# Stores of the FFN's left sums in GpSimd's queue, a residual in two steps, x ahead of single k tiles of weights, and half of tile six's offset by an adding transfer

## The chip, the cores and the metric

The kernel runs on one NeuronCore of one Trainium2 chip. The time is the device time of one execution in microseconds (us); before the change it is 1409.3 us, the median of three runs (1408.26 to 1409.47). Lower is better. Five engines work beside each other, each through its own instructions in order: TensorE (PE in the profile, with PEld for its weight loads), VectorE (DVE), ScalarE (ACT), GpSimd (POOL) and SyncE (SP), which here does nothing but issue DMAs. GpSimd issues some DMAs as well.

## The reference, cut to what matters

One layer of a transformer trunk over 1024 tokens of 1024 channels, in float32. Two attention branches share one input projection, are gated and merged, and a SwiGLU FFN follows; each half ends with a layer norm of a residual sum.

```python
def layer_norm(x, g, b):
    mu = jnp.mean(x, axis=-1, keepdims=True)
    var = jnp.mean(jnp.square(x - mu), axis=-1, keepdims=True)
    return (x - mu) * lax.rsqrt(var + LN_EPS) * g + b

h = x @ w_in                                   # q, k, v of both branches, and two gates
...
mix = (gate_a * y_a + gate_b * y_b) @ w_out
x = layer_norm(DEEPNORM_ALPHA * x + mix, ln1_g, ln1_b)
g, u = jnp.split(x @ w_ffn_in, 2, axis=-1)     # 1024 x (2 * 2816)
ffn = (jax.nn.silu(g) * u) @ w_ffn_out
x = layer_norm(DEEPNORM_ALPHA * x + ffn, ln2_g, ln2_b)
```

## The kernel before

**How a product is made.** Every matrix product runs in a reduced float format in three passes: each float32 operand is split in a high part (ScalarE's copy, a CAST in the profile) and a low part (VectorE subtracts the high part from the source), and TensorE multiplies high by high, high by low and low by high. `split` at lines 108 to 111 is this pair of instructions, so L110 and L111 stand for all splits, and a tile's name tells which. Most products are besides done as 2 by 2 blocks with seven instead of eight block products, from sums and differences of the operand's blocks; the seven steps of a column tile are `p1`, `p2`, `p6`, `p5`, `p7`, `p3`, `p4` in `pair_steps`. Each is 12 matmuls of 128 x 512. `p1`, `p6`, `p7` and `p4` add up in one PSUM bank (`sx`), and between them ScalarE copies the bank out: L202 after `p1`, L211 after `p6`. `p7` can't start until the copy at L211 is done.

**The start.** Column tile 0 of queries and of keys (`project_plain`) is done without the seven products, since its first operands are the first data to arrive. SP issues, in the order of the code, the weights of two k tiles (`w0raw`, 128 x 512) and then x of these two k tiles (`xraw`, 128 x 512 each, the low half of the tokens), four times over, and then the high halves of x. The splits on ScalarE and VectorE are kept in the same order by `in_order`, and TensorE runs k tile by k tile: six matmuls for each.

**The FFN's first product.** `up_steps(f)` makes the column tile f of the hidden layer, f from 1 to 21, and `run_pairs` runs their steps in turn; between two steps it prepares the weights of the next tiles (`right_f`: the sums `taf`, `tbf` and the splits `wbf`, `waf`, `wcf`; `left_f`: the split `wlf`, two tiles ahead). After every second f the two tiles of the hidden layer form a pair q = f // 2, and `left_sums(q)` lists pieces that prepare the second product's left operands: seven operands, each split into a tile `sl` and stored to DRAM (`s_dr`), with four sums between them. `next_piece` takes one piece after each step. The stores are issued by SP, as the loads of the weights are. `sl` takes a buffer of the tag `op` (8 buffers) three times in four, which it shares with `wlf` and `wcf`, and of the tag `kp` (4 buffers) otherwise. A buffer is free again when its store has landed.

**The residual.** Of tile q the scaled residual is built in DRAM: `x1_dr` is filled with the norm's offset at first, and `scale_x1(q, half)`, a piece of its own in the list, loads the normed half tile and the gain (`x1g`, tag `kp`), multiplies them on GpSimd and adds the product to `x1_dr` by an adding DMA. All five are instructions of GpSimd's queue, one behind the other; the multiply (L1362) waits for both loads to land.

**The end.** The second product adds up eight tiles of 128 tokens (`accumulate`, L1595), VectorE takes each sum down from PSUM (L1571) and makes the statistics of the norm (L1208, L1216), GpSimd raises the variance to the power -1/2 (L1217), and `norm_2` applies the norm: VectorE's L1606 subtracts the mean and multiplies by the gain. For tiles six (`x_6`, turn 1, j = 2) and seven VectorE's L1609 multiplies by 1/deviation and adds the offset; for others ScalarE and GpSimd do that. Tile seven's last product is cut in two column pieces of 256 (`d` and `dlast`).

**What sets the order.** Within an engine the framework places the instructions when it builds the program; in the code's order where `in_order` or a chain asks for it, and otherwise by when it reckons them ready. So an edit in one place can move rows elsewhere, and the rows of the built programs tell where each instruction stands.

## Time and profile before

One execution was profiled. Its own time is 1409.1 us; the span from the first to the last instruction that the trace shows is 1407.3 us, and 1.8 us lie around it.

| | |
|---|---|
| time, median of 3 runs | 1409.3 us |
| the profiled execution's own time | 1409.1 us |
| its span | 1407.3 us |
| mean granted TensorE clock | 0.998 |
| DVE busy | 1022.8 us (73%) |
| ACT busy | 716.8 us (51%) |
| POOL busy | 304.9 us (22%) |
| DMA moved | 306.98 MB, mean 218 GB/s |
| of it by GpSimd's queue (q0) | 19.93 MB |
| stores `s_dr<-sl`, issued by SP | 77 of 512 KB |

A row of the profile's timeline reads: start in us, duration in us, engine, line, operation, output <- inputs, shape, how many instructions are merged in the row; and in brackets the time that the engine stood idle before it, with what ended the wait. In other views `x77: 675/685/1782` is a count with the shortest, median and longest duration in ns. "SPq" and "POOLq" stand for the engines' issue of a DMA.

### The profile page before, as it was taken

The numbers are of one execution on the slowest core, as the hardware profiler recorded it, in microseconds if no ns is written. First come the engines' busy times: TensorE is split into PE (matmuls) and PEld (weight loads), VectorE is DVE, ScalarE is ACT, GpSimd is POOL, SyncE is SP. The second block draws the span as 40 slices with busy tenths as digits, with TensorE's granted clock in tenths as the row PEclk, the third lists the DMA queues.
The fourth block names the chain that finished last, engine by engine and source line by source line (L and its number), as shares of the span: only waits on it lengthen the run. The fifth ranks groups of instructions, "written<-read, shape, count | busy, mean of one in ns | idle before, by whom it ended". The sixth has DMA issues, their size and how long they took to land. (4 is left out here: it accounts for less than half of the span.)

```text
span 1407.3 us, 19064 instructions
## 1 busy us (share of the span) xinstructions
PE 1394.2 (99%) x6618; PEld 1160.4 (82%) x6618; DVE 1022.8 (73%) x1653; ACT 716.8 (51%) x1265; POOL 304.9 (22%) x400
## 2 busy tenths in 40 slices
PE   9999999999999999999999999999999999999997
PEld 7878888888888888888888888888888888888886
DVE  8967657545787878977887967767767665947666
ACT  6534344545888788873467644433444443323220
POOL 0000000002555878850122011112111100000032
PEclk9999999999999999999999999999999999999999
DMA  7476567847677478845774556556565539996652
GB/s 255 165 279 231 179 225 299 296 182 253 207 220 207 137 265 264 271 169 191 213 179 140 148 169 206 191 161 218 181 218 192 180 145 342 412 387 236 238 183 90
DMA packets 105665, 306.98 MB, mean 218 GB/s; under 512 B 10833, under 2 KB 27217, under 8 KB 105569
## 3 DMA queue, kind: packets, MB, share of 16 engines
q1 hardware_dynamic: 97824, 285.84, 57.0%
q0 software_dynamic: 7744, 19.93, 6.8%
q8 instruction: 52, 0.85, 0.2%
q14 instruction: 45, 0.36, 0.1%
HBM read 197.69 MB, written 108.56 MB: 218 GB/s over the span
## 5 line engine op out<-in xcount | busy, mean ns | idle before, releaser
L1595 PE MATMUL d<-wd,sl 128*128 128x512 f32 (+1 forms) x924 | 207.7, 387 | 0.0
L1595 PEld LDWEIGHTS d<-wd,sl 128*128 128x128 f32 x924 | 172.3, 188 | 35.4
L110 ACT CAST wd<-wd 128x512 fp32r<-128x512 f32 x77 | 46.0, 621 | 115.3 <-PE d L1595 82.1
L799 POOL TENSOR_TENSOR w_b<-w_b,kp_b 128x511 f32<-128x511 f32 (+3 forms) x96 | 96.1, 1013 | 24.8 <-DVE kp_b L794 18.3
L1571 DVE SCALAR_TENSOR_TENSOR x<-d,x 128x512 f32<-128x512 f32 (+1 forms) x57 | 38.6, 679 | 59.2 <-PE d L1595 59.2
L1217 POOL TENSOR_TENSOR mv<-mv,neghalf 128x1 f32<-128x1 f32 x16 | 15.4, 962 | 285.1 <-DVE mv L1216 280.5
L111 DVE TENSOR_TENSOR sl<-h,sl 128x512 fp32r<-128x512 f32 x77 | 53.3, 700 | 27.1 <-ACT sl L110 27.1
L110 ACT CAST sl<-h 128x512 fp32r<-128x512 f32 x77 | 46.6, 620 | 49.5 <-DMA s_dr<-sl 23.6
L794 DVE TENSOR_TENSOR_SCAN kp_b<-kp_b,ident_ps 128x512 f32<-128x512 f32 (+2 forms) x64 | 56.6, 885 | 20.8 <-ACT kp_b L791 19.8
L1417 PE MATMUL ops<-woh,m 128*128 128x512 f32 x224 | 69.8, 390 | 0.0
L734 POOL MEMSET bias<- 64x64 f32 x2 | 0.3, 144 | 315.0 <-ACT bias L730 315.0
L791 ACT ACTIVATE kp_b<-sc_b 128x512 f32<-128x512 f32 (+3 forms) x96 | 48.4, 504 | 27.9 <-PE sc_b L711 22.0
L111 DVE TENSOR_TENSOR wd<-wd,wd 128x512 fp32r<-128x512 f32 x77 | 52.9, 711 | 5.2 <-ACT wd L110 5.1
L111 DVE TENSOR_TENSOR pt_b<-tp_b,pt_b 128x512 fp32r<-128x512 f32 (+1 forms) x96 | 49.9, 544 | 6.6 <-ACT pt_b L110 5.7
L1360 POOL DMA_DIRECT2D x1g<-n_dr x16 | 9.2, 573 | 203.4 <-DVE wbf2l L111 31.6
L764 POOL TENSOR_SCALAR w_a<-w_a,st_a 128x640 f32<-128x640 f32 (+2 forms) x64 | 42.2, 666 | 48.8 <-PE sc_a L711 26.9
L183 PE MATMUL szf<-x1S73h,wcf 128*128 128x512 f32 x160 | 52.5, 389 | 0.0
L110 ACT CAST pt_b<-tp_b 128x512 fp32r<-128x512 f32 (+1 forms) x96 | 46.6, 503 | 8.0 <-PE tp_b L822 7.7
L1417 PEld LDWEIGHTS ops<-woh,m 128*128 128x128 f32 x224 | 42.1, 188 | 8.6
L759 ACT ACTIVATE w_a<-w_a,st_a 128x640 f32<-128x640 f32 (+2 forms) x64 | 44.7, 700 | 8.5 <-DVE st_a L753 7.1
L792 ACT ACTIVATE w_b<-sc_b 128x511 f32<-128x511 f32 (+3 forms) x96 | 48.3, 504 | 0.0
L822 PE MATMUL tp_b<-ident,w_b 128*128 128x128 f32 x288 | 47.3, 272 | 0.3
(1528 smaller groups left out, 4293.3 us busy)
## 6 DMA issues: line engine op xcount, KB each, us to landing
s_dr<-sl SPq DMA_DIRECT2D x77, 512.0 KB, 4.3
sl<-s_dr SPq DMA_DIRECT2D x77, 512.0 KB, 7.4
wLf<-in_w_ffn_in_dram SPq DMA_DIRECT2D x22, 512.0 KB, 5.8
wRf<-in_w_ffn_in_dram SPq DMA_DIRECT2D x22, 512.0 KB, 3.7
wd<-in_w_ffn_out_dram SPq DMA_DIRECT2D x22, 512.0 KB, 8.1
v_dr<-vc SPq DMA_DIRECT2D x16, 512.0 KB, 3.2
qs<-q_dr SPq DMA_DIRECT2D x16, 512.0 KB, 6.1
kh<-k_dr SPq DMA_DIRECT2D x16, 512.0 KB, 6.2
```

The source lines that it names most:

```text
L110: return (nc.scalar.copy(dst_h, src), nc.vector.tensor_tensor(dst_l, src, dst_h.bitcast(F32), ALU.subtract))
L111: nc.vector.tensor_tensor(dst_l, src, dst_h.bitcast(F32), ALU.subtract))
L183: mm(acc, lw[:, ks], rx, start=(first and kt == i == 0), stop=(kt == 3 and i == 2), skip_group_check=not first)
L759: nc.scalar.activation(s[:, 0:w], s[:, 0:w], AF.Exp, bias=st[:, m:m + 1], scale=-1.0, accum_out=st[:, 2:3])
L764: nc.gpsimd.tensor_scalar(s[:, 0:w], s[:, 0:w], st[:, 3:4], 0.0, ALU.mult, ALU.add)
L791: nc.scalar.activation(kp[:, c0:e], sc[:, 0:n], AF.Sigmoid, scale=-1.0)
L792: nc.scalar.activation(be[:, m0:e], sc[:, m0 - c0:n], AF.Sigmoid)
L794: nc.vector.tensor_tensor_scan(kp[:, 0:e], kp[:, 0:e], ident_ps()[:, 0:e], 0.0, ALU.mult, ALU.add)
L799: nc.gpsimd.tensor_tensor(be[:, m0:e], be[:, m0:e], kp[:, m0 - 1:e - 1], ALU.mult)
L822: ins = tr(tp[:, (qb - lo_q) * P:(qb - lo_q + 1) * P], wt[qb - q0][:, (kb - qb) * P:(kb - qb + 1) * P], ident)
L1417: mm(accs[j], a, b, start=(first and i == n == 0), stop=(i == 3 and n == 2), skip_group_check=not first)
L1595: mm(part, a, b, start=(fresh and i == k == 0), stop=(i == n - 1 and k == 2), skip_group_check=not fresh)
```

## The change

The diff has three parts; line numbers after it are higher by 15 to 46.

```diff
     for j in range(4):
+        if j == 0:
+            x_in((0,), LO)
+            for n in range(2):
+                dma(w0raw[0][:, n * 2 * P:(n + 1) * 2 * P], w_first[0][:, n * 2 * P:(n + 1) * 2 * P])
+            x_in((1,), LO)
+            continue
         dma(w0raw[j // 2][:, (LO, HI)[j % 2]], w_first[j])
...
-        in_order(split(*(t[:, cs] for t in w0hl[j // 2]), w0raw[j // 2][:, cs]))
-        for k in (2 * j, 2 * j + 1):
-            in_order(split_x(k, LO))
+        w = [t[:, cs] for t in (*w0hl[j // 2], w0raw[j // 2])]
+        if j == 0:
+            w0, w1 = ([t[:, n * 2 * P:(n + 1) * 2 * P] for t in w] for n in range(2))
+            in_order((nc.vector.tensor_copy(xh[0][:, LO], x_part(0, LO)),
+                      nc.scalar.copy(w0[0], w0[2])))
+            for hi, lo, src in ((xh[0][:, LO], xl[0][:, LO], x_part(0, LO)), w0):
+                in_order((nc.vector.tensor_tensor(lo, src, hi.bitcast(F32), ALU.subtract),))
+            in_order(split(*w1))
+        else:
+            in_order(split(*w))
+            in_order(split_x(2 * j, LO))
+        in_order(split_x(2 * j + 1, LO))
...
-    h_tiles, pieces = {}, []
+    h_tiles, pieces, last_store = {}, [], []
...
-        t, queue = slot("kp", f"x1g{tt}_{cs.start}"), nc.gpsimd
-        queue.dma_start(t[:, LO], n1_dr[tt][:, cs])
-        queue.dma_start(t[:, HI], rows_of(ln1_g, cs))
-        queue.tensor_tensor(t[:, LO], t[:, LO], t[:, HI], ALU.mult)
-        queue.dma_start(x1_dr[tt][:, cs], t[:, LO], accum_op=ALU.add)
+        box, queue = [], nc.gpsimd
+
+        def load():
+            t = slot("kp", f"x1g{tt}_{cs.start}")
+            box.append(t)
+            queue.dma_start(t[:, LO], n1_dr[tt][:, cs])
+            queue.dma_start(t[:, HI], rows_of(ln1_g, cs))
+
+        def scale():
+            t, = box
+            with tc.issue_after(last_store[0].ins):
+                queue.tensor_tensor(t[:, LO], t[:, LO], t[:, HI], ALU.mult)
+            queue.dma_start(x1_dr[tt][:, cs], t[:, LO], accum_op=ALU.add)
+        return load, scale
...
-                dma(s_dr[g][p][:, i * 1024:(i + 1) * 1024], o.bitcast(F32))
+                last_store[:] = [nc.gpsimd.dma_start(s_dr[g][p][:, i * 1024:(i + 1) * 1024],
+                                                     o.bitcast(F32))]
...
         if q < 8:
-            todo[5:5] = [lambda: scale_x1(q, LO)]
-            todo.append(lambda: scale_x1(q, HI))
+            for at, step in zip((1, 4, 6, 9), (*scale_x1(q, LO), *scale_x1(q, HI))):
+                todo[at] = part(both, todo[at], step)
...
+    def norm_2_split(tt, n):
+        (g, b), t, mv = norm2, acc_t[tt], statistics(f"2_{tt}", n)
+        rows = out[tt * P:(tt + 1) * P]
+        nc.vector.scalar_tensor_tensor(t, t, mv[:, 0:1], g, ALU.subtract, ALU.mult)
+        nc.scalar.activation(t[:, HI], t[:, HI], AF.Copy, scale=mv[:, 2:3])
+        nc.gpsimd.dma_start(rows[:, HI], t[:, HI], accum_op=ALU.add)
+
+        def rest():
+            nc.vector.scalar_tensor_tensor(t[:, LO], t[:, LO], mv[:, 2:3], b[:, LO],
+                                           ALU.mult, ALU.add)
+            dma(rows[:, LO], t[:, LO])
+        return rest
...
+            tied("p", nc.gpsimd.dma_start(out[6 * P:7 * P, HI], rows_of(ln2_b, HI)))
...
-            accumulate(END, j, ((0, 256), (256, HW)), lambda: mark_2(tt, 2, 0, 256))
+            accumulate(END, j, ((0, 256), (256, HW)), lambda: (mark_2(tt, 2, 0, 256), rest()))
```

**At the start**, x of k tile 0 is loaded first, then the weights of k tile 0 and of k tile 1 as two transfers of 128 x 256, then x of k tile 1; the weights' columns are laid out anew to suit (on the host and in `part`). VectorE instead of ScalarE makes the high part of x's k tile 0. On VectorE the first rows before are these:

```order
L267 MEMSET warm_182 128x256
L111 TENSOR_TENSOR w0l0_208<-w0raw0_205,w0h0_207 128x512
L111 TENSOR_TENSOR xl0_190<-xraw0_174,xh0_189 128x512
L111 TENSOR_TENSOR xl1_192<-xraw1_176,xh1_191 128x512
L111 TENSOR_TENSOR w0l0_208<-w0raw0_205,w0h0_207 128x512
L111 TENSOR_TENSOR xl2_194<-xraw2_178,xh2_193 128x512
```

On VectorE the same rows of the change:

```order
L267 MEMSET warm_182 128x256
L305 CAST xh0_189<-xraw0_174 128x512
L308 TENSOR_TENSOR xl0_190<-xraw0_174,xh0_189 128x512
L308 TENSOR_TENSOR w0l0_208<-w0raw0_205,w0h0_207 128x256
L111 TENSOR_TENSOR w0l0_208<-w0raw0_205,w0h0_207 128x256
L111 TENSOR_TENSOR xl1_192<-xraw1_176,xh1_191 128x512
L111 TENSOR_TENSOR w0l0_208<-w0raw0_205,w0h0_207 128x512
L111 TENSOR_TENSOR xl2_194<-xraw2_178,xh2_193 128x512
```

One cast has come in, and the first weight split is in two halves, the first of them behind x's low part; from `xl1` on the order is as before.

**In the FFN**, the 77 stores `s_dr<-sl` are issued by GpSimd. `scale_x1` no longer is two pieces of the list of 13: its load and its multiply ride on the pieces 1, 4, 6 and 9 of a list of 11, and the multiply is placed behind the latest store. On ScalarE, in tile f = 8 with the pieces of q = 3 (`h8` and `gt8` belong to f = 8; `wcf10` and `wlf11h` are weights for f = 10 and 11; `sl3_p` is the operand p of q = 3), these rows stand before:

```order
L110 CAST sl3_2_9318<-h7_9104 128x512
L110 CAST waf9h_9205<-taf9_9195 128x1024
L110 CAST wcf10_9353<-wRf10_9337 128x512
L211 COPY h8_9250<-sxf8_9178 128x512
L215 COPY gt8_9191<-szf8_9253 128x512
L110 CAST sl3_7_9356<-h6_8960 128x512
L110 CAST wlf11h_9377<-wLf11_9375 128x1024
```

On ScalarE at the same place of the change:

```order
L110 CAST sl3_2_9307<-h7_9116 128x512
L110 CAST waf9h_9208<-taf9_9198 128x1024
L110 CAST sl3_5_9273<-h7_9116 128x512
L211 COPY h8_9256<-sxf8_9181 128x512
L110 CAST sl3_7_9328<-h6_8966 128x512
L215 COPY gt8_9194<-szf8_9259 128x512
L110 CAST wcf10_9363<-wRf10_9347 128x512
L110 CAST wlf11h_9384<-wLf11_9382 128x1024
```

`sl3_7` has moved ahead of L215, and `wcf10` behind both. On GpSimd the rows of q = 3 before, all of them:

```order
L1360 DMA x1g3_0_9284<-n1_dr3_130 128x512
L1361 DMA x1g3_0_9284<-in_ln1_g_dram 128x512
L1362 TENSOR_TENSOR x1g3_0_9284<-x1g3_0_9284 128x512
L1363 DMA x1_dr3_138<-x1g3_0_9284 128x512
L1360 DMA x1g3_512_9431<-n1_dr3_130 128x512
L1361 DMA x1g3_512_9431<-in_ln1_g_dram 128x512
L1362 TENSOR_TENSOR x1g3_512_9431<-x1g3_512_9431 128x512
L1363 DMA x1_dr3_138<-x1g3_512_9431 128x512
```

On GpSimd the middle of q = 3 in the change:

```order
L1379 DMA x1g3_0_9219<-n1_dr3_130 128x512
L1380 DMA x1g3_0_9219<-in_ln1_g_dram 128x512
L1379 DMA x1g3_512_9311<-n1_dr3_130 128x512
L1404 DMA s_dr0_5_145<-sl3_5_9273 128x1024
L1385 TENSOR_TENSOR x1g3_0_9219<-x1g3_0_9219 128x512
L1404 DMA s_dr0_2_144<-sl3_2_9307 128x1024
L1386 DMA x1_dr3_138<-x1g3_0_9219 128x512
L1380 DMA x1g3_512_9311<-in_ln1_g_dram 128x512
L1404 DMA s_dr0_7_148<-sl3_7_9328 128x1024
L1404 DMA s_dr0_6_147<-sl3_6_9388 128x1024
```

The stores stand between the residual's loads, its multiply and its adding DMA, and the second half's load has come ahead of the first half's multiply.

**At the end**, the right half of tile six's rows of the output is filled with the norm's offset early on; ScalarE multiplies this half by 1/deviation, and an adding DMA of GpSimd's adds it to the output. VectorE keeps the left half, as an instruction of 128 x 512 placed between tile seven's two column pieces. VectorE's rows before, from the gain of tile six on:

```order
L1606 SCALAR_TENSOR_TENSOR x1_6_11163<-x1_6_11163,mv2_6_12737,ln2g_12180 128x1024
L1571 SCALAR_TENSOR_TENSOR x1_7_11164<-d1_1_3_12029,x1_7_11164 128x256
L1609 SCALAR_TENSOR_TENSOR x1_6_11163<-x1_6_11163,mv2_6_12737,ln2b_12182 128x1024
L1208 BN_STATS bn2_7_12713<-x1_7_11164 128x6
L1571 SCALAR_TENSOR_TENSOR x1_7_11164<-dlast_12763,x1_7_11164 128x256
```

VectorE's rows at the same place of the change:

```order
L1635 SCALAR_TENSOR_TENSOR x1_6_11166<-x1_6_11166,mv2_6_12741,ln2g_12183 128x1024
L1600 SCALAR_TENSOR_TENSOR x1_7_11167<-d1_1_3_12032,x1_7_11167 128x256
L1640 SCALAR_TENSOR_TENSOR x1_6_11166<-x1_6_11166,mv2_6_12741,ln2b_12185 128x512
L1223 BN_STATS bn2_7_12717<-x1_7_11167 128x6
L1600 SCALAR_TENSOR_TENSOR x1_7_11167<-dlast_12769,x1_7_11167 128x256
```

The order is the same; the third row is half as wide.

More of the change, by code (lines that the diff above doesn't have):

```diff
@@ L347, in part @@
         def part(side, half, k, first, last):
-            o = (k // 2 % 2) * HW + side * 2 * P + (k % 2) * P
+            o = (k // 2 % 2) * HW + (k % 2) * 2 * P + side * P
             wh, wl = (t[:, o:o + P] for t in w0hl[k // 4])
@@ L1357, in scale_x1, with both @@
     def scale_x1(tt, cs):
-        t, queue = slot("kp", f"x1g{tt}_{cs.start}"), nc.gpsimd
-        queue.dma_start(t[:, LO], n1_dr[tt][:, cs])
-        queue.dma_start(t[:, HI], rows_of(ln1_g, cs))
-        queue.tensor_tensor(t[:, LO], t[:, LO], t[:, HI], ALU.mult)
-        queue.dma_start(x1_dr[tt][:, cs], t[:, LO], accum_op=ALU.add)
+        box, queue = [], nc.gpsimd
[10 more added lines that the diff above has]
+        return load, scale
+    def both(*steps):
+        for step in steps:
+            step()
     def left_sums(q):
@@ L1665, in hybrid_trunk_kernel @@
             mark_2(tt, 1, 0, HW)
-            norm_2(tt, 2, j > 0)
+            if j == 2:
+                rest = norm_2_split(tt, 2)
+            else:
+                norm_2(tt, 2, j > 0)
 def granules(w):
@@ L1679, in layout @@
     w_in = granules(arr["w_in"])
-    w_first = np.stack([w_in[n].reshape(P, 4, 2 * P) for n in (0, 4)], axis=2)
+    w_first = np.stack([w_in[n].reshape(P, 4, 2, P) for n in (0, 4)], axis=3)
     w_v = np.stack([arr["w_in"][:, c:c + HW] for c in (1024, 2560)], axis=1)
```

2 lines of the change are left out of this document (1 added, 1 removed).

## The prediction

> **What bounds the kernel now.** I read the busy shares first, then TensorE's waits.
>
> ```profile
> PE 1394.2 (99%) x6618; PEld 1160.4 (82%) x6618; DVE 1022.8 (73%) x1653; ACT 716.8 (51%) x1265; POOL 304.9 (22%) x400
> PE sxp L183 <- ACT c L202: 1.3, 1, 1.3
> PE sxf L183 <- ACT h L211: 1.1, 2, 0.8
> PE sxp L183 <- DVE c L198: 0.4, 1, 0.4
> ```
>
> TensorE is busy 99% of the span and its clock is granted at 0.998, so what can go is the time in which it waits or hasn't begun, and the tail. Of the waits (us in total, how often, the longest) 1.3 and 0.4 lie in the projections, which the change doesn't edit. The 1.1 us of `sxf` lie in the FFN. The change touches three places, each with a sum of its own.
>
> **The start.** This is its timeline:
>
> ```profile
> 0.73 0.39 SPq L291 DMA_DIRECT2D w0raw<-in_w_first_dram  x1
> 1.17 0.89 SPq L281 DMA_DIRECT2D xraw<-in_xt_dram  x2
> 3.58 0.62 ACT L110 CAST w0h<-w0raw 128x512 fp32r<-128x512 f32 x1 [1.57 <-DMA w0raw<-in_w_first_dram]
> 4.24 0.62 ACT L110 CAST xh<-xraw 128x512 fp32r<-128x512 f32 x1
> 4.91 0.93 PE L351 MATMUL plain<-xh,w0h 128*128 128x512 f32 x2
> 6.01 0.62 ACT L110 CAST w0h<-w0raw 128x512 fp32r<-128x512 f32 x1 [0.38 <-DMA w0raw<-in_w_first_dram]
> 7.30 1.36 DVE L111 TENSOR_TENSOR xl<-xraw,xh 128x512 fp32r<-128x512 f32 x2
> 8.28 0.39 PE L351 MATMUL plain<-xl,w0h 128*128 128x512 f32 x1
> 84.56 0.41 DVE L330 COPY rel_sb<-rel_in 8x513 f32<-8x513 f32 x1 [3.23 <-DMA wv<-in_w_v_dram]
> ```
>
> The first matmul (4.91) follows two casts of 0.62 on ScalarE, one behind the other, from the first landing at 3.58. After the change x lands first and VectorE casts it while ScalarE casts a half as wide piece of weights. VectorE's cast of 128 x 512 isn't in this trace. It lies between the copy of 513 columns (0.41) and the two-input instruction of 512 (1.36 / 2 = 0.68); I take 0.41, the nearer form, with one input. So x's high part is there at 3.99. The weights' first half is 128 KB behind 256 KB; I let it land 0.4 later than x, from 1.17 - 0.73 between two issues, and its cast takes between 0.31 (half of 0.62) and 0.62, I take 0.4. That gives 3.98 + 0.40 = 4.38, and a first matmul at about 4.4, **0.5 us earlier**.
>
> It doesn't last. VectorE has x's low part (3.99 + 0.68 = 4.67) and the weights' low half (0.4 more, 5.1) in time for these six matmuls, but k tile 2 needs weights that land at 6.01, as late as before, since the bytes ahead of them are the same 768 KB. From there the old order follows: the low part of k tile 2 is done at 7.30 + 1.36 / 2 = 7.98, and the matmul that takes it ran at 8.28. TensorE can be only **0.3 early** there, and later k tiles are no tighter. I take 0.25. Bounds: 0.5 gained if the weights of k tiles 2 and 3 land sooner; 0.14 lost if the added issue (0.44) delays them in full (7.98 + 0.44 - 8.28). The later projection hides nothing of this, since TensorE works without a gap from here to its first wait.
>
> **The FFN.** The two waits are these, with what led to the first:
>
> ```profile
> 931.07 1.22 DVE L111 TENSOR_TENSOR waf9l<-taf,waf9h 128x1024 fp32r<-128x1024 f32 x1
> 938.47 0.62 ACT L110 CAST sl<-h 128x512 fp32r<-128x512 f32 x1 [5.75 <-DMA s_dr<-sl]
> 939.12 0.69 DVE L111 TENSOR_TENSOR sl<-h,sl 128x512 fp32r<-128x512 f32 x1 [3.49 <-ACT sl L110]
> 944.64 1.23 DVE L111 TENSOR_TENSOR wlf11l<-wLf,wlf11h 128x1024 fp32r<-128x1024 f32 x1 [2.90 <-DMA s_dr<-sl]
> 948.91 1.05 ACT L110 CAST wbf10h<-tbf 128x1024 fp32r<-128x1024 f32 x1 [2.25 <-DVE tbf L153]
> 951.33 0.58 ACT L211 COPY h<-sxf 128x512 f32<-128x512 f32 x1
> 951.96 0.50 PE L183 MATMUL sxf<-x1S73h,waf9h 128*128 128x512 f32 x1 [0.82 <-ACT h L211]
> 1104.95 0.50 PE L183 MATMUL sxf<-x1S73h,waf17h 128*128 128x512 f32 x1 [0.32 <-ACT h L211]
> ```
>
> Read backwards: TensorE waited 0.82 for ScalarE's copy at 951.33, which stood behind `wbf10h`, which waited for VectorE's `tbf`, which was late because VectorE sat 2.90 at `wlf11l` until a buffer came free at 944.64 by a store's landing. That store followed a split at 938.47 to 939.8, which itself had waited 5.75 for another store to land. Two landings in a row, each some 4.8 us (939.8 to 944.64), set the stall.
>
> Two things change, as the rows in the section on the change show for this place. The split of `sl3_7` now stands ahead of L215 on ScalarE, where before it stood behind and waited until 938.47; so on VectorE it follows `waf9l` (until 932.3), `sl3_5` and `sl3_2`, and is done at about 932.3 + 3 x 0.69 = 934.4. Its store is GpSimd's, behind two stores, the multiply, an adding DMA and a load:
>
> ```profile
> L1360 POOL DMA_DIRECT2D x1g<-n_dr x16: 566/570/592, 801.8 to 1105.2; - x16
> L1362 POOL TENSOR_TENSOR x1g<-x1g x16: 1274/1286/1792, 806.9 to 1112.3; 128x512 f32<-128x512 f32 x16
> L1363 POOL DMA_DIRECT2D x_dr<-x1g x16: 903/903/929, 809.2 to 1114.0; - x16
> s_dr<-sl SPq DMA_DIRECT2D x77, 512.0 KB, 4.3
> x_dr<-x1g POOLq DMA_DIRECT2D x16, 256.0 KB, 4.2
> x1g<-n_dr POOLq DMA_DIRECT2D x16, 256.0 KB, 5.0
> ```
>
> A plain store by GpSimd isn't in the trace; its issue lies between SP's (0.33 for the output's stores, in the tail's rows) and the adding 0.90, and I take 0.57, from GpSimd's plain load. From `waf9l`'s end (932.3) the queue issues a load 0.57, a store 0.57, the multiply 1.29, a store 0.57, the adding DMA 0.90 and a load 0.57: the store of `sl3_7` goes at 932.3 + 4.5 = 936.8. Landing takes 4.2 to 5.0 by the rows of GpSimd's queue, so it is there at 941.8 at the latest instead of 944.64, **2.8 us earlier**, more than the 0.82 that TensorE lost. A landing would have to take 7.8 us to use all of it up. The same holds at f = 17. GpSimd has the time: 77 x 0.57 = 44 us more, where it idled most of the stage, and SP's loads of weights no longer stand behind stores that wait for VectorE. Of the 1.14 I take **0.8**, since the rows move in every pair and one of them may open a small wait. Bounds: 1.14 gained, and the loss of the first rival.
>
> The Trainium skill, in SBUF — State Buffer, section "SBUF: two separate sides", warns against this move: a DMA of GpSimd's queue needs GpSimd to write its descriptors, and a VectorE instruction that holds the port they share keeps it from that. The trace disagrees for this stage, where VectorE is busy most of the time: the sixteen adding DMAs took 903 to 929 ns each. By the rule each store could be late by an instruction of VectorE's, some 0.7 us, and the FFN's term would still be nearly whole.
>
> **The tail.**
>
> ```profile
> 1388.62 0.55 POOL L1217 TENSOR_TENSOR mv<-mv,neghalf 128x1 f32<-128x1 f32 x1 [3.18 <-DVE mv L1216]
> 1396.84 1.58 POOL L1217 TENSOR_TENSOR mv<-mv,neghalf 128x1 f32<-128x1 f32 x1 [7.68 <-DVE mv L1216]
> 1396.92 2.32 PE L1595 MATMUL dlast<-wd,sl 128*128 128x256 f32 x18
> 1398.46 1.28 DVE L1609 SCALAR_TENSOR_TENSOR x<-x,mv,ln2b 128x1024 f32<-128x1024 f32 x1
> 1400.00 0.41 DVE L1571 SCALAR_TENSOR_TENSOR x<-dlast,x 128x256 f32<-128x256 f32 x1
> 1401.38 1.05 POOL L1217 TENSOR_TENSOR mv<-mv,neghalf 128x1 f32<-128x1 f32 x1 [2.95 <-DVE mv L1216]
> 1402.60 1.41 DVE L1609 SCALAR_TENSOR_TENSOR x<-x,mv,ln2b 128x512 f32<-128x512 f32 x2
> L1614 SPq DMA_DIRECT2D out_dram<-x x9: 332/332/338, 1361.3 to 1404.0; - x9
> out_dram<-x SPq DMA_DIRECT2D x2, 256.0 KB, 2.0
> ```
>
> TensorE ends at 1396.92 + 2.32 = 1399.24, but VectorE takes the last sum only at 1400.00, 0.76 late, behind tile six's L1609 of 1.28. Half as wide it takes 0.7 (1.41 / 2), so 0.58 goes; all behind it is one chain on VectorE and GpSimd to the last store at 1404.0. I take **0.55**. What replaces the right half lies beside it: ScalarE's multiply of 128 x 512 (idle there; about 0.6 from 1398.46), then GpSimd's adding DMA from 1399.1, 0.90 long, which is over at 1400.0, before the next power is due at 1401.38 - 0.55 = 1400.8. It lands at 1399.1 + 4.2 = 1403.3, ahead of the last stores, issued until 1403.45 and landed at 1405.45. If its issue is stretched beside VectorE as the power is (1.58 against 0.55), it ends at 1401.0 and the power is 0.2 late. Bounds: 0.76 gained, all of the lateness, to 0.1 lost, if the adding DMA lands 7 us after its issue and closes the kernel.
>
> **Sum:** 0.25 + 0.8 + 0.55 = 1.6 off the profiled execution's own 1409.1, so 1407.5. The median of the runs is 0.2 above that execution; the forecast on the median's scale is **1407.7**.
>
> **Rivals.** *GpSimd's multiply slows VectorE's chain (slower).* Where L1362 ran beside VectorE, a VectorE instruction got longer:
>
> ```profile
> 919.16 1.29 POOL L1362 TENSOR_TENSOR x1g<-x1g 128x512 f32<-128x512 f32 x1 [5.41 <-DMA x1g<-in_ln_g_dram]
> 919.25 1.74 DVE L1337 TENSOR_TENSOR h<-h,gt 128x512 f32<-128x512 f32 x1
> 931.19 0.58 ACT L211 COPY h<-sxf 128x512 f32<-128x512 f32 x1
> 931.93 0.40 PE L183 MATMUL sxf<-x1S73h,waf8h 128*128 128x512 f32 x1
> ```
>
> 1.74 instead of 0.69 (the split at 939.12 has the same form): 1.05 lost. The multiply now goes right behind a store whose split stands in a burst of VectorE's, so it will meet one nearly every time. The slack is small: the copy at 931.19 ended at 931.77, 0.16 before TensorE took the bank at 931.93. If the 1.05 falls ahead of ScalarE's casts and thereby of that copy, each of 8 pairs costs 1.05 - 0.16 = 0.9, 7 in all, against the start's and the tail's 0.8: 1409.3 + 6.3 = **1415.6**; met in only three pairs, with the FFN's old waits left, 1409.3 - 0.8 + 2.7 = **1411.2**. It decides once a stretched instruction lies between `taf` and the copy L211; at f = 8 it lies behind `waf9l`, which speaks against it. The Trainium skill (SBUF — State Buffer, "SBUF: two separate sides") calls the shared port an exclusive lock between a GpSimd instruction that reads SBUF and a VectorE one with two inputs there; the rows agree.
>
> *The stores land no earlier.* In-order issue behind multiplies, loads that wait for buffers and slow landings use up the 2.8 us; the FFN's waits stay and the change doesn't do there what it says: 1409.3 - 0.8 = **1408.5**.
>
> *More waits go.* If the reordering also removes the projections' 1.3, and every term reaches its upper bound, 1409.3 - 0.5 - 1.14 - 0.76 - 1.3 = **1405.6**.
>
> **How the numbers follow.** Chances: forecast 0.51, stores no earlier 0.25, the slow rival 0.16 (0.08 mild, 0.08 in full), more waits 0.08. A measurement of this kernel tells about 0.2% from no change, 2.8 us: below 1406.5 is faster, above 1412.1 slower. The forecast and the second rival lie within it; of the mild slow cases half reach past it. So faster 0.08, same 0.80, slower 0.12. The range goes from 1406.0, where all three terms reach their upper bounds with a little of the projections' waits, to 1411.2, the mild slow case.
>
> **What would show it.** First matmul near 4.4 and k tile 2's second near 8.0; no wait of `sxf` for ACT `h` at f = 9 and 17; `wlf` waits for `s_dr` shorter; the last sum taken at TensorE's end plus 0.2; the adding DMA of tile six landed before the last store. Wrong would be: VectorE instructions of 1.7 in every pair followed by waits of `sxf`; GpSimd's stores landing nearly 8 us after issue; the adding DMA as the last to land.

## The result: 11.9 us slower

| | median us | lowest to highest | executions |
|---|---|---|---|
| before | 1409.38 | 1408.26 to 1409.63 | 6 |
| after | 1421.30 | 1418.59 to 1422.63 | 6 |

The ratio is 1.0084, with a 95% interval from 1.0071 to 1.0097. The profiled execution of the changed kernel took 1421.56 us; its span is 1419.8 us, against 1407.3. The forecast of 1407.7 and its range, which ended at 1411.2, are both missed.

Three views of the changed kernel: the busy times from its page, with the group of the stores from the view by lines; TensorE's waits (us in total, how often, the longest); and the timeline of its start (us from the span's start, duration, and in brackets the idle time ahead and what ended it).

```profile
PE 1398.2 (98%) x6618; PEld 1159.7 (82%) x6618; DVE 1023.4 (72%) x1655; ACT 716.5 (50%) x1266; POOL 355.0 (25%) x479
L1404 POOL DMA_DIRECT2D s_dr<-sl x77 | 44.1, 582 | 309.3 <-DVE sl L111 286.6 <-DVE x L1600 8.2 <-DVE wd L1580 7.3
```

```profile
PE sxf L183 <- ACT h L211: 4.8, 4, 1.7
PE szf L183 <- ACT gt L215: 4.2, 6, 1.4
PE plain L366 <- ACT xh L110: 0.8, 1, 0.8
PE sxf L183 <- ACT gt L202: 0.6, 1, 0.6
```

```profile
3.56 0.43 DVE L305 CAST xh<-xraw 128x512 fp32r<-128x512 f32 x1 [2.44 <-DMA xraw<-in_xt_dram]
4.40 0.91 PE L366 MATMUL plain<-xh,w0h 128*128 128x512 f32 x1
6.62 0.62 ACT L110 CAST xh<-xraw 128x512 fp32r<-128x512 f32 x1 [1.13 <-DMA xraw<-in_xt_dram]
7.29 0.49 PE L366 MATMUL plain<-xh,w0h 128*128 128x512 f32 x1 [0.81 <-ACT xh L110]
```

The waits of `sxf` and `szf` come to 9.5 us where 1.1 stood, and those of `szf` are new. To place the loss I counted TensorE's matmuls in both traces (6618 each) and compared the start of the same one. The matmul that ran at 8.28 before now runs at 9.52. Number 4000, at the beginning of the FFN's pairs, ran at 807.7 and now runs at 809.4; number 5400, near their end, at 1126.9 and now at 1140.1. So 1.24 us are lost at the start, 0.4 more on balance in the projections and the attention, **11.6 in the FFN** (330.7 us for that stretch, against 319.2), and between 5400 and TensorE's last group nothing changes. From that group's start to the end of the span it takes 9.64 us instead of 10.41.

The FFN's waits grew by 8.4 us, its time by 11.6. The rest is there as well, but a wait doesn't show it: a matmul starts 0.227 us after the one before it (the median), while its record lasts 0.39, so the first 0.16 us of a delay are not idle time. Counted from start to start, 25 steps of that stretch take over 0.3 us, where 4 did, and together they are 12.9 us longer than median steps, against 1.7.

What the FFN's new waits are made of is seen in one of those for L215, on ScalarE, GpSimd and TensorE of the changed kernel (timeline):

```profile
996.80 0.54 POOL L1404 DMA_DIRECT2D s_dr<-sl  x1 [11.93 <-DVE sl L111]
997.35 1.32 POOL L1385 TENSOR_TENSOR x1g<-x1g 128x512 f32<-128x512 f32 x1
997.65 0.58 ACT L211 COPY h<-sxf 128x512 f32<-128x512 f32 x1
998.13 1.15 ACT L110 CAST sl<-h 128x512 fp32r<-128x512 f32 x2
1001.57 0.62 ACT L110 CAST wcf<-wRf 128x512 fp32r<-128x512 f32 x1 [2.29 <-DMA s_dr<-sl]
1002.09 0.58 ACT L215 COPY gt<-szf 128x512 f32<-128x512 f32 x1
1002.72 0.50 PE L183 MATMUL szf<-x1S73h,wcf 128*128 128x512 f32 x1 [1.42 <-ACT gt L215]
```

and at the same place of the kernel before (f = 11):

```profile
987.66 0.59 ACT L211 COPY h<-sxf 128x512 f32<-128x512 f32 x1
988.14 1.14 ACT L110 CAST sl<-h 128x512 fp32r<-128x512 f32 x2
990.38 0.59 ACT L215 COPY gt<-szf 128x512 f32<-128x512 f32 x1 [1.09 <-PE szf L183]
992.08 0.62 ACT L110 CAST wcf<-wRf 128x512 fp32r<-128x512 f32 x1 [1.11 <-DMA s_dr<-sl]
```

Read the four ScalarE rows in both. Before, the copy L215 waits only for TensorE's product, and the cast `wcf`, which needs a buffer that a store's landing frees, comes behind it and hurts nobody when it waits. After, the two have changed places: the cast waits 2.29 us for a landing, L215 stands behind it in ScalarE's in-order queue, and TensorE waits 1.42 us for L215. The store that is waited for is not late in its queue: it went out at 996.80, 0.4 us after VectorE had its split done, and landed 4.7 us later.

The six waits for L215 come to 4.2 us. The four for L211, 4.8 us, come another way, by VectorE, as the wait did that the prediction had read in the kernel before. This is the one just ahead of the rows above:

```profile
978.05 3.74 POOL L1385 TENSOR_TENSOR x1g<-x1g 128x512 f32<-128x512 f32 x1
984.01 0.86 POOL L1404 DMA_DIRECT2D s_dr<-sl  x1
990.84 1.23 DVE L111 TENSOR_TENSOR wlf13l<-wLf,wlf13h 128x1024 fp32r<-128x1024 f32 x1 [5.92 <-DMA s_dr<-sl]
995.23 1.06 ACT L110 CAST wbf12h<-tbf 128x1024 fp32r<-128x1024 f32 x1 [3.18 <-DVE tbf L153]
998.29 0.50 PE L183 MATMUL sxf<-x1S73h,waf11h 128*128 128x512 f32 x1 [1.23 <-ACT h L211]
```

VectorE had the split of the store at 984.01 done by 980.03, but GpSimd was at a multiply of 3.74 us, and a load and an adding transfer followed it in the queue. VectorE stood 5.92 us at `wlf13l` until the store had landed (1.04 at the same place before), so `tbf`, ScalarE's `wbf12h` and behind it L211 came late. The other three go alike: the cast `wbf` waits 1.9 to 3.1 us for `tbf`, and VectorE had stood 3.2 to 6.0 us before it, twice at `wlf` until a store had landed and once at `wcf`, whose cast waited for one.

### The profile page after: what moved, and what is told of

Its sections match the earlier page's. It is cut to its first block, busy times and chain, and to the rows that moved or that the text cites. A ratio compares the mean times of both kernels' runs of the same rounds, so it can differ in the third digit from the quotient of the medians.

```text
span 1419.8 us, 19067 instructions
## 1 busy us (share of the span) xinstructions
PE 1398.2 (98%) x6618; PEld 1159.7 (82%) x6618; DVE 1023.4 (72%) x1655; ACT 716.5 (50%) x1266; POOL 355.0 (25%) x479
## 5 line engine op out<-in xcount | busy, mean ns | idle before, releaser
L1404 POOL DMA_DIRECT2D s_dr<-sl x77 | 44.1, 582 | 309.3 <-DVE sl L111 286.6
L110 ACT CAST wd<-wd 128x512 fp32r<-128x512 f32 x77 | 45.4, 620 | 108.3 <-PE d L1624 92.0
L837 PE MATMUL tp_b<-ident,w_b 128*128 128x128 f32 x288 | 47.3, 272 | 0.2
```

What stands on the lines that cost most here:

```text
L110: return (nc.scalar.copy(dst_h, src), nc.vector.tensor_tensor(dst_l, src, dst_h.bitcast(F32), ALU.subtract))
L837: ins = tr(tp[:, (qb - lo_q) * P:(qb - lo_q + 1) * P], wt[qb - q0][:, (kb - qb) * P:(kb - qb + 1) * P], ident)
L1404: last_store[:] = [nc.gpsimd.dma_start(s_dr[g][p][:, i * 1024:(i + 1) * 1024], o.bitcast(F32))]
```

## The experiments

All kernels are the kernel before with a part of the change, some with an edit of that part. A ratio is to the kernel before, run beside it.

### The three parts alone

The tail alone, twice, then the start alone, then the FFN part alone; the edits are the diff's hunks for that part.

> The kernel before with the change's tail alone (tile six's right half by ScalarE and GpSimd's adding transfer). In the profile of the changed kernel the last sum was taken 0.23 us after TensorE's end, against 0.76 before, and behind TensorE's last instruction nothing else was longer. So the tail alone gives 0.5 to 0.7 us: about 1408.8 us against 1409.4. The rival, that the adding transfer's landing closes the kernel, gives no gain or a loss: the gap between the last landing and TensorE's end is then as long as before.

> The kernel before with the change's tail alone, a second time, since the first interval (0.9986 to 1.0003) leaves open whether it is faster. By the term of the tail (0.53 us less between TensorE's end and the last sum) 0.3 to 0.9 us faster than before, ratio about 0.9995; the two intervals together should lean to below 1. If it is nothing, the ratio is 1.0000 and more.

> The kernel before with the change's start alone (x ahead, the first weights in two pieces of 128 KB). If the 1.25 us that the changed kernel's start lost comes from the order and the number of the transfers, it is there again: first matmul at 4.4, x's k tile 1 cast only at about 6.6, TensorE 1.2 to 1.3 us behind from its 21st matmul on, and the whole kernel at about 1410.6 us. If it was an accident of the one profiled execution, k tile 1 is there at about 5.1 and the kernel takes 1409.1 us. The projections' first waits (94.78 before, 1.3 us) may take some of it back.

> The kernel before with the change's FFN part alone, nothing of the start and the tail: the part whose share has so far been worked out from the whole. If the three parts add up (start +1.6, tail -0.9 as measured alone), it takes 1421.3 - 1.6 + 0.9 = 1420.6 us less what the two medians of before differ by, 1419 to 1421 us, with the same waits of sxf and szf at the same matmuls. If the start's loss had pushed the FFN into another order of events, it is 1414 us or less.

| part | us | before beside it | ratio, 95% |
|---|---|---|---|
| tail | 1408.13 | 1409.03 | 0.9994 (0.9986 to 1.0003) |
| tail again | 1407.73 | 1408.63 | 0.9993 (0.9984 to 1.0001) |
| start | 1410.67 | 1409.03 | 1.0011 (1.0003 to 1.0020) |
| FFN part | 1419.38 | 1408.71 | 1.0074 (1.0059 to 1.0089) |

The parts add up: -0.9 + 1.6 + 10.7 = 11.4 of the 11.9. The tail's gain is too small for one interval, but both medians are 0.9 below, and its rows move as forecast (below). The start's loss is there again: k tile 1 of x is cast at 6.47, and the matmul of 8.28 runs at 9.36. But a part of that is chance of the one profile of before: in the 14 profiles whose start is that of before, it ran at 8.10 to 9.40, with 8.70 in the middle, and k tile 1 was cast at 4.92 to 6.51. The FFN part alone shows the same kind of waits, 4.3 us of `sxf` for L211 and 3.6 of `szf` for L215.

### Which part of the FFN's edit

First the two halves of the edit, each without the other. Stores in SyncE's queue, residual in two steps:

```diff
-                last_store[:] = [nc.gpsimd.dma_start(s_dr[g][p][...], o.bitcast(F32))]
+                last_store[:] = [nc.sync.dma_start(s_dr[g][p][...], o.bitcast(F32))]
```

> The kernel before with the change's FFN part, but the stores of the left sums back in SyncE's queue: the residual's two steps alone. Theory 1 (GpSimd's queue works in order, and stores in it stand behind loads of x1g that wait for a buffer and behind multiplies that wait for those loads to land): the loss of 11.6 us in the FFN is gone, 1408.5 to 1410.5 us. Theory 2 (two tiles of x1g are live at a time and take buffers that the weights' sums need, whatever queue the stores are in): most of the loss stays, 1416 to 1421 us. Theory 3 (GpSimd's multiplies run longer beside VectorE and lengthen its instructions): the multiplies still stand in the middle of VectorE's work, and 1411 to 1420 us, by how many of them last 3.7 us.

Stores in GpSimd's queue, residual in one step:

```diff
-            for at, step in zip((1, 4, 6, 9), (*scale_x1(q, LO), *scale_x1(q, HI))):
-                todo[at] = part(both, todo[at], step)
+            todo[5:5] = [part(both, *scale_x1(q, LO))]
+            todo.append(part(both, *scale_x1(q, HI)))
```

> The kernel before with the stores of the left sums in GpSimd's queue, and the residual in one step at its old place (load, load, multiply, adding transfer in one piece). Theory 1 (stores wait in GpSimd's in-order queue): the multiply now waits in that queue for its own loads, 5 us and more, with stores behind it, so the loss stays or grows: 1419 to 1440 us, with waits of ScalarE's casts for the stores' landings as long or longer than in the changed kernel. Theory 2 (two live tiles of x1g): the loss is gone, 1409 to 1411 us. Theory 3 (multiplies that meet VectorE): they are back where before had them, at most 1411 us.

Measured: 1411.42 us (ratio 1.0017, 1.0004 to 1.0030) and 1435.72 us (1.0184, 1.0171 to 1.0197). Most of the loss goes with the stores' queue, as the first theory has it, though the 12 executions of the first kernel lie far apart (1408.15 to 1417.97 us). It has one large stall of its own (timeline of the kernel with SyncE's stores):

```profile
1102.42 0.69 DVE L152 TENSOR_TENSOR tbf<-wRf,taf 128x512 f32<-128x512 f32 x1 [7.21 <-DMA x_dr<-x1g]
1107.40 0.63 PE L183 MATMUL sxf<-x1S73h,waf17h 128*128 128x512 f32 x1 [3.87 <-ACT h L211]
```

There `tbf` waits for the adding transfer that frees a buffer of `kp`: the second theory, at one place of the whole FFN.

Then what GpSimd's queue holds beside the stores: no residual at all (its four steps taken off the list), or only the multiply taken out:

```diff
-            with tc.issue_after(last_store[0].ins):
-                queue.tensor_tensor(t[:, LO], t[:, LO], t[:, HI], ALU.mult)
```

> The kernel before with the change's FFN part, and the residual's steps left out (loads of x1g, multiplies, adding transfers: the first norm's scaled rows are missing from the sum). GpSimd's queue then holds the stores alone. Theory 1 (stores stand behind steps of the residual that wait): the loss of 11.6 us is gone, 1407.5 to 1409.5 us, and the stores go out within 0.7 us of their splits. Rival (a store that GpSimd issues is itself slower, 0.58 us of issue against 0.32, and lands later): at least 5 us of the loss stay, 1414 to 1420 us.

> The kernel before with the change's FFN part, and only the 16 multiplies on GpSimd left out (the rows are added unscaled). Theory 1: the loads of x1g still wait in GpSimd's queue for a buffer, and the adding transfer for the loads' landing, with stores behind both, so most of the loss stays, 1416 to 1421 us. Theory 3 (multiplies that run 3.7 us beside VectorE and lengthen its instructions): the loss is gone, 1409 to 1411 us.

Without the residual 1409.20 us (1.0009, 0.9999 to 1.0018), with every store issued within 0.7 us of its split: the loss of over 10 us is gone, though the stores are still GpSimd's. By the interval at most 2.5 us stay; the kernel also lacks the residual's transfers, so this isn't the price of the stores alone. Without the multiply 1441.84 us (1.0240, 1.0221 to 1.0260), 34 us more than before, with GpSimd's adding transfers now waiting for the loads:

```profile
POOL x_dr L1369 <- DMA x1g<-n_dr: 32.0, 12, 5.0
```

Taking the multiplies out made it worse, since what follows them in the queue came forward and waited. So this kernel doesn't tell what the multiplies themselves cost. In the changed kernel they did last longer (29.4 us for 16, against 21.4 before), and one of the three over 3.7 us stands in the chain shown above.

Two kernels that should have mended it by the first theory: the loads of x1g in SyncE's queue, and the residual behind the last store of each pair.

```diff
-            queue.dma_start(t[:, LO], n1_dr[tt][:, cs])
-            queue.dma_start(t[:, HI], rows_of(ln1_g, cs))
+            dma(t[:, LO], n1_dr[tt][:, cs])
+            dma(t[:, HI], rows_of(ln1_g, cs))
```

> The kernel before with the change's FFN part, but the residual's loads of x1g in SyncE's queue; GpSimd keeps the stores, the multiplies and the adding transfers. Theory 1: no store stands behind a load any more, so ScalarE's casts no longer wait long for the stores' landings; of the 11.6 us at least 8 go, 1408.5 to 1412.5 us, unless the loads, waiting for a buffer, now hold up the loads of weights behind them in SyncE's queue: then TensorE waits for weights (wRf, wLf by way of taf, tbf or wlf), and that is seen in the waits. If the loss follows from the stores' queue or the two live tiles, whatever queue the loads are in, it stays, 1417 us and more.

```diff
-            for at, step in zip((1, 4, 6, 9), (*scale_x1(q, LO), *scale_x1(q, HI))):
-                todo[at] = part(both, todo[at], step)
+            (load_0, scale_0), (load_1, scale_1) = scale_x1(q, LO), scale_x1(q, HI)
+            todo.append(part(both, load_0, load_1, scale_0, scale_1))
```

(its loads are tied behind the pair's last store as well)

> The kernel before with the change's FFN part, all in GpSimd's queue, but the residual's four steps moved behind the last store of each pair, its loads too. Theory 1: only the next pair's first stores can stand behind steps that wait, so most of the loss goes, 1408.5 to 1411 us. Theory 2 (two tiles of x1g live at a time, both now): waits for a kp buffer at the sums of weights (taf, tbf), as the one of 3.9 us with the stores in SyncE's queue, 1411 to 1416 us.

Measured: 1414.15 us (1.0043, 1.0030 to 1.0057) and 1427.98 us (1.0138, 1.0124 to 1.0152). The second is a plain miss of the first theory, and it is over the second theory's range too: only one store there goes out more than 3 us behind its split, against 13 in the changed kernel (the end of each store's issue set against the end of its split in the trace), and it is slower than the change. TensorE's waits of the kernel with the loads in SyncE's queue are a single row,

```profile
PE szf L183 <- ACT gt L215: 6.6, 8, 1.5
```

eight waits, all for L215, all behind a cast that waited for a landing. In the kernel with the residual last, VectorE's sums and ScalarE's casts wait for the buffers that the residual itself holds (waits, then a row of ScalarE's timeline):

```profile
PE sxf L183 <- ACT h L211: 11.8, 8, 4.7
DVE taf L151 <- DMA x_dr<-x1g: 3.3, 2, 2.1
```

```profile
1057.93 0.62 ACT L110 CAST sl<-h 128x512 fp32r<-128x512 f32 x1 [5.50 <-DMA x_dr<-x1g]
```

The last row is a cast of a left sum that holds ScalarE for 5.50 us until an adding transfer has landed; `wbf15h` and then L211 stand behind it.

### The order on ScalarE

So a fourth theory was tried by itself: not how late the stores are, but what stands behind the casts that wait for them. One tie puts the left sums' casts behind the copy L215 that is ahead of them in the program:

```diff
         def p5():
             begin("sz", "sc", 5)
-            nc.scalar.copy(c("22"), st["sz"])
+            last_22[:] = [nc.scalar.copy(c("22"), st["sz"])]
...
-                split(o[:, LO], o[:, HI], src)
+                with tc.issue_after(last_22[0].ins):
+                    split(o[:, LO], o[:, HI], src)
```

> The kernel before with the change's FFN part, and one tie on ScalarE: the cast of a left sum (L110, sl) is put behind the copy L215 of the pair's step 5 that stands ahead of it in the program. In the changed kernel six waits of szf, 4.2 us together, came from copies L215 that stood on ScalarE behind a cast (sl or wcf) that waited for a store's landing. Theory 4 (that order is a part of the loss of its own): those waits go, and TensorE's waits in the FFN fall from 9.5 to about 5, 1415 to 1417 us. Theory 1 alone (stores late behind the residual's steps, whatever the order on ScalarE): the waits move to the copies L211 or L202, the sum stays at 9 or more, 1419 to 1422 us.

> As the run before it (the copies L215 ahead of the left sums' casts), and the loads of x1g in SyncE's queue. With the loads there and without the tie all of TensorE's waits in the FFN, 6.6 us, were of szf for L215. Theory 4: they go, and with them nearly all of the loss, 1408.5 to 1410.5 us. If the casts' waits for the stores' landings delay TensorE in another way, it stays at 1412 us or more, with waits of sxf in place of those of szf.

Measured: 1409.75 us (1.0010, 1.0000 to 1.0019) and 1409.95 us (1.0011, 1.0001 to 1.0020). Stores, queue and residual are the change's; of the 10.7 us of the FFN part **9.6 are gone**. TensorE's waits there with the tie:

```profile
PE szf L183 <- ACT gt L215: 0.8, 1, 0.8
PE sxf L183 <- ACT h L211: 0.7, 1, 0.7
PE sxf L183 <- DVE gt L198: 0.5, 1, 0.5
```

More went than the fourth theory expected: the waits for L211 as well. The tie also moves the casts, and with them the stores: three go out over 3 us behind their splits where 13 or 14 did, and no multiply lasts over 1.93 us. These effects are not told apart by this run. The one wait of `szf` that is left is at a place where the cast `wcf`, which isn't tied, still stands ahead:

```profile
993.07 0.62 ACT L110 CAST wcf<-wRf 128x512 fp32r<-128x512 f32 x1 [3.85 <-DMA s_dr<-sl]
993.60 0.58 ACT L215 COPY gt<-szf 128x512 f32<-128x512 f32 x1
994.23 0.50 PE L183 MATMUL szf<-x1S73h,wcf 128*128 128x512 f32 x1 [0.77 <-ACT gt L215]
```

Is the order all of it? The same tie in the kernel of 1435.72 us (residual in one step), and, as the change's best form, with the tail and without the start:

> The stores in GpSimd's queue and the residual in one step (the kernel of 1435.7 us), with the copies L215 tied ahead of the left sums' casts on ScalarE. If that order is the cause by which late stores reach TensorE, most of its 26.7 us go: 1409 to 1416 us. If late stores reach TensorE through the buffers of the weights (wlf, taf, tbf) whatever stands ahead on ScalarE, at least half stays: 1422 us or more.

> The changed kernel with its start undone and the copies L215 tied ahead of the left sums' casts: the FFN part with the tie (1.0 us slower than before when alone) and the tail (0.9 us faster when alone). If they add up, 1408.8 us beside 1408.7 of before, a ratio of 1.0000, and the tail alone stays the best of all. If the two FFN waits that the tie left (0.7 and 0.8 us) were of the one execution, it is 0.9 us or more faster than before, ratio 0.9993 or less.

Measured: 1422.22 us (1.0092, 1.0078 to 1.0106) and 1408.55 us (1.0001, 0.9992 to 1.0010). In the first, half of 26.7 us stays, and the waits are others:

```profile
PE sxf L183 <- ACT h L211: 6.9, 5, 2.8
PE sxf L183 <- ACT gt L202: 2.2, 2, 1.4
PE sxf L183 <- DVE gt L198: 1.0, 2, 0.7
```

No wait for L215 is left. Three of the nine stalls can be followed back to their beginning, and that is a store in GpSimd's queue behind a multiply that waited for its loads; from there they come by way of casts and splits of `wlf` and `sl`, whose buffers the stores free.

So there are two ways from a late landing to TensorE: through ScalarE's order to L215, and through the buffers of the weights to L211 and L202. In the change as made TensorE's waits are 4.2 us by the first and 5.3 by the second; with the loads in SyncE's queue all are by the first, with the one-step residual and the tie none. The following table has three counts of the FFN, all from the profiled executions: the casts of `sl` or `wcf` that stand right ahead of a copy L215 and began within 0.1 us of a store's landing, having waited for it; of the 21 copies L215 those that started more than 2.1 us after TensorE had finished their product; and TensorE's waits.

| kernel | such casts ahead of L215 | copies L215 over 2.1 us late | TensorE's waits, us |
|---|---|---|---|
| before | 0 | 0 | 1.1 |
| after | 9 | 7 | 9.5 |
| FFN part alone | 9 | 8 | 8.4 |
| loads in SyncE's queue | 9 | 8 | 6.6 |
| stores in SyncE's queue | 0 | 1 | 4.1 |
| no residual | 8 | 1 | 1.9 |
| no multiply | 9 | 7 | 23.0 |
| residual last | 9 | 5 | 13.7 |
| with the tie | 1 | 1 | 1.9 |
| one-step residual | 6 | 3 | 21.0 |
| one-step residual, tie | 0 | 1 | 10.1 |

The row without the residual shows that the order alone does little. Eight casts wait right ahead of L215 there too, for 0.9 to 3.6 us, but L215 comes at most 2.52 us after its product, and TensorE waits for it once, 0.4 us. In the changed kernel it comes up to 5.03 us after; there a copy 1.91 us late still cost nothing, and one 2.31 us late cost 0.23. So the order uses up some 2 us that TensorE can spare, and what goes beyond them is added where stores share GpSimd's queue with the residual's steps. Without those steps (1409.20 us), or with the tie (1409.75 us), nearly all of the loss is gone. That the tie does it by the order alone isn't shown.

The change with tie and tail is as fast as before, no faster than the tail alone: nothing of the FFN's edit is a gain that these runs show. By the medians the tail alone is the fastest kernel of this study, and its two intervals (to 1.0003 and 1.0001) just fail to exclude no difference.

### The start

x's k tile 0 first, but the weights in one transfer; the two pieces of the weights by ScalarE's queue (with the tail); and four pieces of 64 KB:

```diff
-            for n in range(2):
-                dma(w0raw[0][:, n * 2 * P:(n + 1) * 2 * P], w_first[0][:, n * 2 * P:(n + 1) * 2 * P])
+            dma(w0raw[0][:, LO], w_first[0])
```

> The kernel before with the change's start, but the first weights in one transfer of 256 KB: x's k tile 0 first, then the weights, then x's k tile 1, which is the third transfer again, as before. If the loss comes from the added transfer's issue (0.47 us, which puts k tile 1 in the fourth place), k tile 1 lands by 5.0 us as before, TensorE has its 21st matmul at 8.0 to 8.4, and the kernel takes 1409.0 us. If it comes from x standing ahead of the weights, the 21st matmul stays at about 9.4 and the kernel at 1410.5 us.

```diff
-                dma(w0raw[0][:, n * 2 * P:(n + 1) * 2 * P], ...)
+                nc.scalar.dma_start(w0raw[0][:, n * 2 * P:(n + 1) * 2 * P], ...)
```

> The kernel before with the change's tail and start, but the two pieces of the first weights are issued by ScalarE's queue beside SyncE's, so that x's k tile 1 is SyncE's second transfer. If the issues one behind the other set the start, k tile 1 is there by 4.5 us, TensorE keeps the 0.3 us that it is early at its 9th matmul and has its 21st at 7.9 to 8.1, and the kernel takes 1407.8 us (0.3 from the start, 0.9 from the tail, as the tail alone measured). If the half pieces themselves or x ahead of the weights slow the start, the 21st matmul is at 9.0 or later and the kernel at 1409 us or more.

```diff
-            for n in range(2):
-                dma(w0raw[0][:, n * 2 * P:(n + 1) * 2 * P], w_first[0][:, n * 2 * P:(n + 1) * 2 * P])
+            for n in range(4):
+                dma(w0raw[0][:, n * P:(n + 1) * P], w_first[0][:, n * P:(n + 1) * P])
```

> The kernel before with the change's start, and the first weights in four transfers of 64 KB instead of two of 128 KB, so that x's k tile 1 is the sixth transfer instead of the fourth. If a transfer's place in the row of issues (0.47 us each) sets its landing whatever its size, k tile 1 comes 0.9 us later than with two pieces, at about 7.4 us, TensorE has its 21st matmul at 10.2 to 10.5, and the kernel takes about 1411.5 us. If the bytes ahead set it, or chance, k tile 1 lands at 5.0 to 6.6 and the 21st matmul comes at 8.3 to 9.5.

Measured: 1408.04 us (1.0001, 0.9991 to 1.0010), 1408.07 us (1.0001, 0.9993 to 1.0010) and 1411.42 us (1.0018, 1.0009 to 1.0027). The matmul of 8.28 (the expectations' 21st, counted from 0 with the eight that warm TensorE up) ran at 9.07, 9.04 and 9.50. In time, the weights in one transfer cost nothing that can be measured, and the pieces in SyncE's queue cost 1.6 and 2.8 us. The kernel with two queues has the tail in it; without the tail's 0.9 its start costs about 1.1 us, an estimate from the medians. But no theory of the place in the row of issues holds: with four pieces k tile 1 was issued 0.94 us later than with two and was cast at 6.61, as with two (6.62 and 6.47), and a second issuing queue brought nothing: x's k tile 0 was cast at 4.37, later than in any other kernel that loads x first. (With four pieces the first matmul came at 6.12, since ScalarE's table load, 1.28 us, had fallen behind the wait for the first weights.) What differs is how much arrives in the first 5 us (the transfers' view; before, after, and with the two pieces in ScalarE's queue):

```profile
DMA packets 534, 0.99 MB, mean 197 GB/s; under 512 B 53, under 2 KB 53, under 8 KB 534
```

```profile
DMA packets 524, 0.70 MB, mean 140 GB/s; under 512 B 54, under 2 KB 310, under 8 KB 524
```

```profile
DMA packets 675, 0.98 MB, mean 196 GB/s; under 512 B 68, under 2 KB 324, under 8 KB 675
```

With pieces the packets are smaller (those under 2 KB go from 53 to 310 and 324). In SyncE's queue a quarter to a third fewer bytes are there than in the 14 profiles with the start of before (0.83 to 1.04 MB), in ScalarE's queue no fewer. So the packets' size alone doesn't do it; what does stays open.

Nor does the time hang on the first matmuls alone. In one kernel with the start of before (the one without the multiply, whose loss is all in the FFN) the matmul of 8.28 ran at 9.40, as late as with the pieces, and yet number 400 at 95.79, where before had it at 96.05: TensorE's wait of 1.3 us, which lies between (94.8), was gone. What the pieces add lies ahead of that wait. From matmul 100 to 300 (26 to 72 us in before) the 14 kernels with the start of before take 45.4 to 45.7 us, and the one with the weights in one transfer 45.4; the changed kernel and the start alone take 46.8, the kernel with two queues 46.4 and that with four pieces 47.3. In these four, rows of the projections stand in another order. The changed kernel, and before:

```profile
60.93 1.22 DVE L406 SCALAR_TENSOR_TENSOR c<-c,hi 128x1024 f32<-128x1024 f32 x1
63.27 1.22 DVE L406 SCALAR_TENSOR_TENSOR c<-c,hi 128x1024 f32<-128x1024 f32 x1
64.40 1.22 DVE L111 TENSOR_TENSOR wbp3l<-tbp,wbp3h 128x1024 fp32r<-128x1024 f32 x1
65.68 0.50 PE L183 MATMUL sxp<-s24h,wbp3l 128*128 128x512 f32 x1 [0.34 <-DVE wbp3l L111]
```

```profile
60.48 1.22 DVE L391 SCALAR_TENSOR_TENSOR c<-c,hi 128x1024 f32<-128x1024 f32 x1
61.62 1.22 DVE L111 TENSOR_TENSOR wbp3l<-tbp,wbp3h 128x1024 fp32r<-128x1024 f32 x1
```

Both instructions of 1.22 us now stand ahead of `wbp3l`, which TensorE waits for; before, the second stood behind it. So some 1.2 us of the start's loss (46.8 against 45.6) are again rows that moved. No run has the pieces without the new order, so what each costs in time isn't told apart.

## Why the prediction was wrong, by its steps

**The start (forecast -0.25, bounds -0.5 to +0.14; measured +1.6 in time; in the trace, at the matmul of 8.28, +1.24 against the profile of before and +0.8 against the middle of 14).** The first matmul came at 4.40, as worked out. Two steps failed. The first is "k tile 2 needs weights that land at 6.01, as late as before, since the bytes ahead of them are the same 768 KB". It was not the weights that TensorE waited for but x's k tile 1, for which the sum had no term: cast at 6.62 and 6.47, where profiles with the start of before have 4.92 to 6.51. And equal bytes didn't arrive in equal time, for a reason that stays open. The second is "From there the old order follows". The first rows on VectorE do follow it, but from 41 us on ScalarE's and VectorE's rows differ again, and some 1.2 us are lost there.

**The FFN (forecast -0.8; measured +10.7 alone).** Of the two old waits, those for L211 at f = 9 and 17 are gone, as forecast; TensorE waits for L215 there instead, 0.23 and 0.58 us. `wlf11l` waits less (before 2.90):

```profile
938.39 1.22 DVE L111 TENSOR_TENSOR waf9l<-taf,waf9h 128x1024 fp32r<-128x1024 f32 x1
944.78 0.92 POOL L1404 DMA_DIRECT2D s_dr<-sl  x1
951.07 1.23 DVE L111 TENSOR_TENSOR wlf11l<-wLf,wlf11h 128x1024 fp32r<-128x1024 f32 x1 [2.12 <-DMA s_dr<-sl]
```

But the store of `sl3_7` was forecast to land 2.8 us earlier, and counted from the end of `waf9l` (939.61) it landed 0.9 us earlier. It went out 5.2 us after that end instead of 4.5, since the multiply took 1.99 us and not 1.29, and landed 6.3 us later. The 4.2 to 5.0 that were called the latest are medians of transfers half as large; the changed kernel's 77 stores took 2.9 to 9.3 us.

A store's issue was priced at 0.57 and took 582 ns in the mean. The Trainium skill warns, in SBUF — State Buffer, section "SBUF: two separate sides", that GpSimd can't write a DMA's descriptors while VectorE runs an instruction in a two-port mode. These 582 ns show nothing of it. VectorE's instructions in the FFN's stretch (807 to 1160 us) are all TENSOR_TENSOR, 333 of them, and no run shows the mode they ran in, so the warning isn't put to the test here. With the stores alone in that queue (no residual) the time could not be told from before.

The step that failed is the allowance for the order: "the rows move in every pair and one of them may open a small wait", 0.34 us. Eleven waits came, 9.5 us in all and up to 1.7 us each. "The split of `sl3_7` now stands ahead of L215 on ScalarE" was read as a gain, an earlier store; that L215, which TensorE waits for, then stands behind a cast that can wait for a landing was left out. At f = 8, the tile that was looked at, the cast didn't wait and L215 came in time. At the odd f from 3 to 19, nine times, it stood right behind a cast of `sl` or `wcf` that waited 1.3 to 3.2 us. The Trainium skill says, in Perfetto Trace Analysis, section "Tensor Engine Instruction (MATMUL, LD_WEIGHTS)", that ScalarE, VectorE and GpSimd work strictly first in, first out; the trace agrees, with L215 starting at 1002.09, right behind a cast that had kept ScalarE idle for 2.29 us. This is 4.2 of the 9.5 us. The other 5.3 come by the path that the prediction had followed itself, from a store's landing over VectorE to L211 or L202, at tiles that it hadn't looked at: there the stores landed late enough to open it anew.

**The rivals.** The slow rival had the right sign and the wrong mechanism: the multiply met VectorE and lasted up to 3.7 us itself, while VectorE's busy time grew by 0.6 us only (1023.4 against 1022.8, with two instructions more). "The stores land no earlier" was nearly right about the stores and took it for harmless.

**The tail (forecast -0.55).** Right. The last sum is taken 2.55 us after the last group's start, where it was 3.08 (1396.92 to 1400.00), the power that follows isn't stretched, 1.05 as before, and the adding transfer landed at 1416.78, ahead of the last store at 1418.76:

```profile
1410.15 2.32 PE L1624 MATMUL dlast<-wd,sl 128*128 128x256 f32 x18
1412.70 0.41 DVE L1600 SCALAR_TENSOR_TENSOR x<-dlast,x 128x256 f32<-128x256 f32 x1
1412.85 0.91 POOL L1637 DMA_DIRECT2D out_dram<-x  x1 [1.19 <-ACT x L1636]
1414.09 1.05 POOL L1232 TENSOR_TENSOR mv<-mv,neghalf 128x1 f32<-128x1 f32 x1 [0.33 <-DVE mv L1231]
```

The 0.53 us of the trace stand beside 0.9 in the medians of both runs of the tail alone, whose intervals reach from a gain of 2 us to none.

## What to carry to other kernels

When a transfer changes its queue, look first at what the scheduler then changes on the engines that wait for buffers, and at every tile, not at the one that the edit was made for. An instruction that can wait for a landing and stands ahead of the one that the busiest engine waits for uses up that engine's slack, and anything that delays the landing then costs time; one tie may be worth more than the queue. An order that shows a row moved forward has to be read for what was pushed behind it, too. And an edit at the start can move rows far behind it: here the order changed again 40 us later.

## What the runs showed of the hardware

A GpSimd multiply of 128x512 that took 1274 to 1792 ns before took up to 3765 ns beside VectorE's splits, in the changed kernel:

```profile
L1385 POOL TENSOR_TENSOR x1g<-x1g x16: 1284/1342/3765, 821.4 to 1115.8; 128x512 f32<-128x512 f32 x16
```

What these long multiplies cost by themselves isn't shown.

In the first 5 us, with the weights and x in transfers of 256 KB, 0.83 to 1.04 MB arrived (15 profiles); with one of the transfers cut in two in the same queue it was 0.65 and 0.70 MB, and with the two pieces in a second queue 0.98 MB. And the same code at the start had x's k tile 1 cast up to 1.6 us apart from one kernel to the next.
